# A decoder layer in float32: the normalisation factors of two layer boundaries spread by two float32r products in place of one float32 product, with the work around them in another order

## The chip, the cores and the metric

The kernel runs on one core of a Trainium2 chip. The core has a matrix engine (TensorE, "PE" in the profile; its weight loads are listed as "PEld"), three engines for elementwise work (VectorE "DVE", ScalarE "ACT", GpSimd "POOL") and DMA queues, of which SyncE ("SP") issues most. Each engine works through its own list of instructions in the order in which the program has them; between engines semaphores say when an operand is ready. The metric is the device time of one execution in microseconds (us), lower is better.

## What is computed

One layer of a decoder on 512 tokens of 1024 features, in float32: a gated feed-forward layer (FFN), a token mixer, and another FFN. Each has an RMS normalisation ahead of it and one behind it:

```python
for l in range(DEPTH):                       # DEPTH = 1
    x = x + 0.5 * rms_norm(swiglu(rms_norm(x, ffn1_pre_g[l]), ...), ffn1_post_g[l])
    y = hybrid_mixer(rms_norm(x, mix_pre_g[l]), ...)
    x = x + rms_norm(y, mix_post_g[l])
    x = x + 0.5 * rms_norm(swiglu(rms_norm(x, ffn2_pre_g[l]), ...), ffn2_post_g[l])

def rms_norm(x, g):
    return x * rsqrt(mean(x * x, axis=-1, keepdims=True) + 1e-6) * g
```

The mixer projects the 1024 features to an RG-LRU branch, its gate, and queries, keys and values, and ends in a 1024x1024 product `w_o`. What follows is about the two **boundaries**: from the output of the first FFN to the input of the mixer, and from the output of the mixer to the input of the second FFN. There a block's output `y` is normalised, added to the residual stream `xT`, and the next block's input is made from the sum.

## The kernel before

Activations lie transposed: a tile has 128 features on the partitions and the 512 tokens along the free axis, so `y`, `xT` and the next input are eight **chunks** (0 to 7) of 128 features each. The tokens come in two halves of 256 (`HALF`).

**Products.** A float32 product is made of three products in float32r, a rounded form of float32: each operand is split into a high part (rounded to float32r) and a low part (what is left), and high*high, high*low and low*high are added up in PSUM (`mm3`, lines 512 to 514). For weights ScalarE makes the high part (a CAST, line 210) and VectorE or GpSimd subtracts it for the low part (line 215). The class `Weights` holds these units in the order of their use; `W.fill(n)` has the casts and subtractions of the next n units issued at that point of the program, `W.round()` only the next cast. A unit whose low part is `shared` is cast in two halves, and VectorE and GpSimd take half of the subtraction each (line 195).

**A boundary** (`boundary`, called once per boundary; `parts` is given at the first and None at the second). The last three chunks of `y` (5, 6, 7; `late`) are computed first for token half 0 and then for token half 1, each as a product of 18 matmuls (first boundary) or 24 (second) of 256 columns. After each, VectorE copies or adds the result into `y` (`late`), ScalarE squares it (`late_square`), and VectorE adds the square to a running sum (`late_add`). When the sum of a half is complete, the class `InvRms` takes four steps:

- `stats`: TensorE sums the squares over the 128 partitions with a column of 1/1024 (`mean_d`, line 558; a float32 product, so each call runs as two instructions, four for the half);
- `invert`: ScalarE takes the square root (line 564), VectorE the reciprocal (line 566), and VectorE writes two 128x128 diagonal matrices of the factors, `dg`, beside each other (line 568);
- `spread`: TensorE multiplies a 128x128 matrix of ones by `dg` (line 572), which puts the factor of each token on every partition. This product is float32 too, and runs as two instructions of 256 columns;
- per chunk: VectorE scales `y` by gain and factor (`scale`, line 749), VectorE (even chunks) or GpSimd (odd chunks) adds it to `xT` (`add`, line 753), ScalarE makes the high part of the next input `xh` from it (`high`, line 618), and later VectorE the low part `xl` (line 621).

TensorE then starts the first four products of the next block (tiles `an` at the first boundary, `mn` at the second) with the high parts alone, chunk by chunk (`k_high`, lines 530 and 531: eight matmuls per chunk): chunks 0 to 3 of token half 0, the `stats` of half 1, chunks 4 and 5, the `spread` of half 1, chunks 6 and 7, and then all eight chunks of half 1. The low parts follow (`k_low`, line 537).

In the kernel before, `stats` of half 0 stands in the middle of the product of chunk 6, half 1, and `spread` of half 0 ahead of the product of chunk 7, half 1. Behind the spread the chunks go in pairs: two scales, the VectorE add, then the two high parts. The order of all this is the order of the Python code: nothing reorders the instructions of an engine.

## Time and profile before

| what | value |
| --- | --- |
| device time, three runs | 836.93, 837.26, 837.74 us (median 837.26) |
| device time of the profiled execution | 837.42 us |
| its span, from the first to the last instruction | 835.6 us |
| TensorE busy | 827.5 us, 99% of the span |
| VectorE, ScalarE, GpSimd busy | 732.7, 518.8, 165.9 us |
| granted TensorE clock, mean | 0.998 |
| the first boundary's late products and first next products | about 328 to 366 us of the span |
| the second boundary's | about 480 to 523 us |

A row of the timeline has the start, the duration, the engine, the line and operation, and the tiles written and read; in brackets stands the idle time ahead of it and what ended that. Rows of equal instructions that follow each other are merged (x2, x4), with the time from the first start to the last end. TensorE's matmuls overlap: a 256-column matmul is listed with 0.28 us, but one starts every 0.12 us, so what a product costs is read from the distance of starts. Line numbers in the text are those of the kernel before.

### The profile page before, as it was taken

The page shows a single profiled execution, that of the slowest core. Times are in us where ns is not written, and L with a number is a line of the kernel's source. Part 1 is how long each engine was busy: PE and PEld are TensorE (multiplying, and loading weights), DVE is VectorE, ACT ScalarE, POOL GpSimd, SP SyncE. Part 2 cuts the span into 40 slices and gives each one's busy share as a digit, 9 for nine tenths or more (in the row PEclk, how much of TensorE's full clock was granted, in tenths as well). Part 3 has the DMA queues.
Part 4 walks back from the last instruction along what each step waited for, and adds up shares of the span by engine and source line. Part 5 has one row for each costly group of instructions (what it writes and reads, how often), then busy time and mean ns, then how long its engine had stood idle before and what let it go on. Part 6 is the DMA issues. An engine that isn't in the chain of part 4 may idle for free.

```text
span 835.6 us, 11875 instructions
## 1 busy us (share of the span) xinstructions
PE 827.5 (99%) x4244; PEld 704.3 (84%) x4244; DVE 732.7 (88%) x1035; ACT 518.8 (62%) x806; POOL 165.9 (20%) x188
## 2 busy tenths in 40 slices
PE   9999999999999999999999999999999999999996
PEld 8988888888888898987788899888888888888885
DVE  4989799998989977888789689998999799898996
ACT  6656756676666654556897446545757677676562
POOL 2022000140320325414521052002005023032001
PEclk9999999999999999999999999999999999999999
DMA  7376408398595897522511140566339939769742
GB/s 253 103 272 231 151 12 308 89 266 259 128 260 179 187 282 244 170 79 93 167 42 51 51 130 23 126 176 253 118 110 243 311 91 256 234 156 259 301 141 101
DMA packets 121851, 144.22 MB, mean 173 GB/s; under 512 B 24184, under 2 KB 76736, under 8 KB 121280
## 3 DMA queue, kind: packets, MB, share of 16 engines
q1 hardware_dynamic: 107824, 112.91, 42.2%
q0 software_dynamic: 13824, 30.42, 16.6%
q8 instruction: 33, 0.54, 0.3%
q14 instruction: 26, 0.21, 0.1%
q10 hardware_dynamic: 144, 0.13, 0.0%
HBM read 100.45 MB, written 39.32 MB: 167 GB/s over the span
## 4 chain that ended last, share of the span: by engine, by line
PE 98%; DMA 1%; DVE 0%; SPq 0%; issue 0%; DVEq 0%
PE aa L999 10%; PE ab L999 10%; PE db L999 5%; PE da L999 5%; PE yaa L1390 3%; PE ba L999 3%; PE bb L999 3%; PE ya L1390 3%; PE yda L1390 2%; PE aa L929 1%; PE a_first L1260 1%; PE yab L1981 1%; PE yab L1979 1%; PE yab L1980 1%; PE wo L1905 1%; PE gt L512 1%
## 5 line engine op out<-in xcount | busy, mean ns | idle before, releaser
L1171 POOL DMA_DIRECT2D yr_a<-stage x36 | 31.6, 1020 | 176.5 <-ACT stage L1168 156.0
L1171 POOL DMA_DIRECT2D yp_b<-stage x42 | 36.5, 1065 | 146.8 <-ACT stage L1168 118.4
L1995 POOL DMA_DIRECT2D yp_b<-stage x8 | 4.3, 546 | 64.9 <-ACT stage L1994 64.4
L722 POOL TENSOR_TENSOR acca_r<-acca_r,sq_r 128x512 f32<-128x512 f32 x6 | 8.6, 1430 | 39.7 <-ACT sq_r L542 39.6
L530 PE MATMUL an<-xh_mx,whi_xl 128*128 128x256 f32 x64 | 15.9, 289 | 0.0
L531 PE MATMUL an<-xh_mx,wlo_xl 128*128 128x256 f32 x64 | 15.5, 283 | 0.0
L2098 POOL TENSOR_TENSOR last<-yp,grow 128x512 f32<-128x512 f32 x3 | 3.9, 1292 | 56.5 <-DVE yp L2088 56.5
L2095 ACT ACTIVATE ysq<-yp 128x512 f32<-128x512 f32 (+1 forms) x8 | 4.9, 607 | 15.7 <-DVE yp L2088 15.7
L512 PE MATMUL gt<-xh_mx,whi_gt 128*128 128x512 f32 x32 | 14.3, 446 | 0.0
L1427 POOL DMA_DIRECT2D yp_a<-zy x16 | 8.7, 554 | 25.0 <-DMA rows_a<-yr_a 16.7
L512 PE MATMUL pq<-xh_mx,whi_q 128*128 128x512 f32 x32 | 12.8, 401 | 0.0
L514 PE MATMUL gt<-xh_mx,wlo_gt 128*128 128x512 f32 x32 | 12.6, 394 | 0.0
L512 PE MATMUL pgb<-xh_f,whi_bg 128*128 128x512 f32 x32 | 12.6, 393 | 0.0
L513 PE MATMUL gt<-xl_mx,whi_gt 128*128 128x512 f32 x32 | 12.5, 391 | 0.0
L514 PE MATMUL pq<-xh_mx,wlo_q 128*128 128x512 f32 x32 | 12.5, 391 | 0.0
L514 PE MATMUL pgb<-xh_f,wlo_bg 128*128 128x512 f32 x32 | 12.5, 390 | 0.0
L514 PE MATMUL pub<-xh_f,wlo_bu 128*128 128x512 f32 x32 | 12.5, 390 | 0.0
L513 PE MATMUL pq<-xl_mx,whi_q 128*128 128x512 f32 x32 | 12.5, 390 | 0.0
L513 PE MATMUL pub<-xl_f,whi_bu 128*128 128x512 f32 x32 | 12.5, 390 | 0.0
L512 PE MATMUL pub<-xh_f,whi_bu 128*128 128x512 f32 x32 | 12.5, 390 | 0.0
L513 PE MATMUL pgb<-xl_f,whi_bg 128*128 128x512 f32 x32 | 12.5, 389 | 0.0
L1390 PE MATMUL ya<-whi_ad,hha 128*128 128x512 f32 x32 | 12.5, 389 | 0.0
(2038 smaller groups left out, 3414.3 us busy)
## 6 DMA issues: line engine op xcount, KB each, us to landing
yp_b<-stage POOLq DMA_DIRECT2D x50, 256.0 KB, 9.0
yr_a<-stage POOLq DMA_DIRECT2D x44, 256.0 KB, 9.6
h_a<-za SPq DMA_DIRECT2D x16, 256.0 KB
h_b<-zb SPq DMA_DIRECT2D x16, 256.0 KB
hxb<-h_b SPq DMA_DIRECT2D x16, 256.0 KB
hxa<-h_a SPq DMA_DIRECT2D x6, 512.0 KB
xn<-in_x SPq DMA_DIRECT2D x8, 256.0 KB
raw_ad<-in_ffn_w_down SPq DMA_DIRECT2D x2, 1024.0 KB
```

The lines of the kernel that those rows point to most:

```text
L512: pe.matmul(ps, hi[:, k, :], xh, start=start, stop=False)
L513: pe.matmul(ps, hi[:, k, :], xl, start=False, stop=False)
L514: pe.matmul(ps, lo[:, k, :], xh, start=False, stop=stop)
L530: pe.matmul(ps[:, sl], hi[:, k, :], xh, start=k == 0 and not goes_on, stop=False, skip_group_check=True)
L531: pe.matmul(ps[:, sl], lo[:, k, :], xh, start=False, stop=False, skip_group_check=True)
L722: eng.tensor_add(acc, acc, square(part, ALL, f"{self.name}{c}"))
L929: pe.matmul(o, w[:, k, js], x, start=first and i + j + k == 0, stop=k == 3 and i == 2, skip_group_check=True)
L999: pe.matmul(b[tb], x[:, blk], w[:, k, :], start=first and q + k + j == 0, stop=q + k == 2 and j == 2, skip_group_check=True)
L1171: pool.dma_start(o, st, accum_op=ALU.add)
L1260: pe.matmul(banks[j][:, HALF[0]], ws[j][part][:, k, :], n1.xs[k][xpart][:, HALF[0]], start=k == 0 and part == xpart, stop=stop and k == KD ...
L1390: pe.matmul(o, x[:, blk], a[:, k, :], start=start and j == 0, stop=stop and j == 2, skip_group_check=True)
L1427: (pool if q % 2 else sync).dma_start(chunks[32 * q:32 * (q + 1), :, i * P:(i + 1) * P], turned[32 * i:32 * (i + 1), :, q])
```

## The change

All of it concerns the two boundaries.

1. `invert` also rounds the factor to float32r (`rh`), subtracts (`rl`), and writes two diagonals into one tile: that of the factor (rounded on writing) and that of its rest. `spread` is two float32r products with ones, summed in PSUM.
2. At the second boundary, for half 0, the sum of squares itself is split into a high and a low part (`apart`: a ScalarE cast and a VectorE subtraction), and `stats` is four float32r products with a two-column `mean_r`.
3. The spread of half 0 moves two steps of k (six matmuls) into the product of chunk 7, half 1 (`SPREAD = 2`). Right behind it chunk 0 alone is scaled, added and rounded, then chunk 1; the result of chunk 6 is copied and squared after chunk 1's scale. Pairs are taken apart in both halves: scale, add and high part of an even chunk, then those of the odd chunk.
4. At the first boundary `W.fill(4)` moves from behind `stats` of half 0 to the start of that product. At the second `W.round` is put there, so the last unit is cast ahead of `stats`, and the fill stays behind.
5. The weights of the second FFN's first two chunks (`bg`, `bu`; four units): before, VectorE subtracts one and GpSimd three; now VectorE subtracts three and half of the fourth, GpSimd the other half.

The diff, cut to its core:

```diff
+SPREAD = 2
...
-        g, u = (add_cols(w_gu[:, :, o:o + F], f, KD, f"{name}{s}", 0, (dve, dve) if f else (dve if s == "g" else pool, pool))
-                for s, o in (("g", 0), ("u", F)))
+        lows = {"g": (dve, pool), "u": (pool, pool)} if name == "a" and not f else {"g": (dve, dve), "u": (dve, dve if f else shared)}
+        g, u = (add_cols(w_gu[:, :, o:o + F], f, KD, f"{name}{s}", 0, lows[s]) for s, o in (("g", 0), ("u", F)))
...
         def stats(self):
...
+                if self.two:
+                    for j, a in enumerate(self.two):
+                        pe.matmul(ps[:, 2 * i:2 * i + 2], a[:, i * P:(i + 1) * P], mean_r, start=j == 0, stop=j == 1)
+                    continue
...
+        def apart(self):
+            a = self.accs[0][:, HALF[self.half]]
+            t = wt(f"two_{self.name}", T, F32R)
+            self.two = hi, lo = t[:, HALF[0]], t[:, HALF[1]]
+            act.copy(hi, a)
+            dve.tensor_sub(lo, a, hi.bitcast(F32))
...
             dve.reciprocal(rs, rms)
-            self.dg = wt(f"dg_{n}", T)[:, :2 * P].rearrange("p (a b) -> p a b", a=2)
-            dve.tensor_tensor(self.dg, ident.unsqueeze(1).to_broadcast([P, 2, P]), rs.unsqueeze(2).to_broadcast([P, 2, P]), op=ALU.mult)
+            dve.tensor_copy(high, rs)
+            dve.tensor_sub(low, rs, high.bitcast(F32))
+            self.dg = wt(f"dg_{n}", T, F32R)
+            for d, r in zip(HALF, (rs, low)):
+                dve.tensor_tensor(self.dg[:, d].rearrange("p (a b) -> p a b", a=2), ident.unsqueeze(1).to_broadcast([P, 2, P]),
+                                  r.unsqueeze(2).to_broadcast([P, 2, P]), op=ALU.mult)
 
         def spread(self):
             o = self.ps[:, T // 2:]
-            pe.matmul(o, ones.bitcast(F32), self.dg.rearrange("p a b -> p (a b)"), start=True, stop=True)
+            for i, d in enumerate(HALF):
+                pe.matmul(o, ones, self.dg[:, d], start=i == 0, stop=i == 1)
...
+            if i == LATE - 1 and parts is None:
+                res.rms[0].apart()
             W.fill((2, 3, 3)[i])
...
-        def spread_a():
+        def first():
             spread(0)
-            steps((0, 1), 0, bcs[0])
-
-        n = len(xs)
-        hooks = [{}, {n // 2: res.rms[0].stats, n // 2 + 1: lambda: W.fill(4)}, {0: spread_a}]
+            step(0, 0, dve)
+            nxt.high(0, 0)
+            res.scale(1, 0, bcs[0])
+            after(1)
+            add(1, 0, pool)
+            nxt.high(1, 0)
+
+        fill = lambda: W.fill(4)
+        hooks = [{}, {1: fill, n // 2: res.rms[0].stats} if parts else {1: W.round, n // 2: res.rms[0].stats, n // 2 + 1: fill}, {SPREAD: first}]
...
         spread(1)
         for k in range(0, KD, 2):
-            steps((k, k + 1), 1, bcs[1])
+            step(k, 1, dve)
+            nxt.high(k, 1)
+            res.scale(k + 1, 1, bcs[1])
+            add(k + 1, 1, pool)
+            nxt.high(k + 1, 1)
```

Here `step(k, h, eng)` is a scale and an add, and `after(i)` the copy and the square of late chunk i.

How this moves instructions is shown at three places. First ScalarE at the first boundary, from the square of chunk 5, half 1 (`sq_r`), to the first high parts (`xh_mx`); `rms_sr` is the square root, `whi_xl` a weight's high part. Before:

```order
L542 ACTIVATE sq_r_3353<-yp_a_3131 128x256
L564 ACTIVATE rms_sr_3369<-rms_r_3366,eps 128x2
L210 CAST whi_xl_1_3378<-raw_xl__3185 128x512 x2
L542 ACTIVATE sq_r_3394<-yp_a_3131 128x256
L618 ACTIVATE xh_mx_3243<-xT_3180,cols 128x256
L618 ACTIVATE xh_mx_3245<-xT_3180,cols 128x256
```

And now, on the same engine at the same place:

```order
L545 ACTIVATE sq_r_3355<-yp_a_3133 128x256
L211 CAST whi_xl_1_3362<-raw_xl__3187 128x512 x2
L580 ACTIVATE rms_sr_3380<-rms_r_3377,eps 128x2
L638 ACTIVATE xh_mx_3245<-xT_3182,cols 128x256
L545 ACTIVATE sq_r_3414<-yp_a_3133 128x256
L638 ACTIVATE xh_mx_3247<-xT_3182,cols 128x256
L638 ACTIVATE xh_mx_3249<-xT_3182,cols 128x256
```

The two casts now stand ahead of the square root, and the first high part ahead of the square of chunk 6. Second, VectorE at the same place, from the running sum (`accb_r`) to the first add into `xT`; `rs_r` is the reciprocal, `wlo_xl` the VectorE half of a weight's low part. Before:

```order
L741 TENSOR_TENSOR accb_r_3066<-acca_r_3065,sq_r_3353 128x256
L566 RECIPROCAL rs_r_3371<-rms_sr_3369 128x2
L568 TENSOR_TENSOR dg_r_3373<-ident,rs_r_3371 128x256
L195 TENSOR_TENSOR wlo_xl_1_3379<-raw_xl__3185,whi_xl_1_3378 128x512
L728 TENSOR_TENSOR yp_a_3131<-ay_3356,yp_a_3131 128x256
L749 SCALAR_TENSOR_TENSOR yp_a_2971<-yp_a_2971,half_g,rms_r_3366 128x256 x2
L753 TENSOR_TENSOR xT_3180<-yp_a_2971,xT_3180 128x256
```

And now, with the rounded factor `rh_r`, its rest `rl_sr` and the second diagonal:

```order
L761 TENSOR_TENSOR accb_r_3068<-acca_r_3067,sq_r_3355 128x256
L196 TENSOR_TENSOR wlo_xl_1_3363<-raw_xl__3187,whi_xl_1_3362 128x512
L581 RECIPROCAL rs_sr_3381<-rms_sr_3380 128x2
L582 CAST rh_r_3383<-rs_sr_3381 128x2
L583 TENSOR_TENSOR rl_sr_3382<-rs_sr_3381,rh_r_3383 128x2
L586 TENSOR_TENSOR dg_r_3388<-ident,rs_sr_3381 128x256
L586 TENSOR_TENSOR dg_r_3388<-ident,rl_sr_3382 128x256
L769 SCALAR_TENSOR_TENSOR yp_a_2973<-yp_a_2973,half_g,rms_r_3377 128x256
L788 TENSOR_TENSOR xT_3182<-yp_a_2973,xT_3182 128x256
L769 SCALAR_TENSOR_TENSOR yp_a_2973<-yp_a_2973,half_g,rms_r_3377 128x256
L748 TENSOR_TENSOR yp_a_3133<-ay_3358,yp_a_3133 128x256
```

The weight's half now stands ahead of the reciprocal, three instructions are new, and chunk 0's add follows its own scale. Third, VectorE at the second boundary, between the first low part (`wlo_bg_0`) and the copies of the late chunks (`y_r`). Before:

```order
L215 TENSOR_TENSOR wlo_bg_0_4930<-raw_bg__4788,whi_bg_0_4929 128x1024
L732 COPY y_r_4962<-my_4937 128x256
L745 TENSOR_TENSOR accb_r_4678<-accb_r_4678,sq_r_4964 128x256
L732 COPY y_r_4998<-my_4973 128x256
L745 TENSOR_TENSOR accb_r_4678<-accb_r_4678,sq_r_5000 128x256
L732 COPY y_r_4923<-my_5003 128x256
```

And now, where `two_r` is the low part of the sum of squares that `stats` reads:

```order
L216 TENSOR_TENSOR wlo_bg_0_4944<-raw_bg__4802,whi_bg_0_4943 128x1024
L216 TENSOR_TENSOR wlo_bu_0_4948<-raw_bu__4862,whi_bu_0_4947 128x1024
L752 COPY y_r_4976<-my_4951 128x256
L765 TENSOR_TENSOR accb_r_4692<-accb_r_4692,sq_r_4978 128x256
L216 TENSOR_TENSOR wlo_bg_1_4982<-raw_bg__4802,whi_bg_1_4981 128x1024
L752 COPY y_r_5012<-my_4987 128x256
L765 TENSOR_TENSOR accb_r_4692<-accb_r_4692,sq_r_5014 128x256
L574 TENSOR_TENSOR two_r_5017<-accb_r_4692,two_r_5017 128x256
L752 COPY y_r_4937<-my_5020 128x256
```

Two low parts that GpSimd had stand between the copies now, and a subtraction follows the last sum.

More of the change, by code (lines that the diff above doesn't have):

```diff
@@ L482, in tile_layer @@
     mean_c = filled("mean_c", 1, 1.0 / C)
+    mean_r = const.tile([P, 2], F32R, name="mean_r")
+    dve.memset(mean_r.bitcast(F32), 1.0 / D)
     eps = filled("eps", 1, EPS)
@@ L550, in __init__ @@
         def __init__(self, accs, mean, half, name, eps=eps):
-            self.accs, self.mean, self.half, self.name, self.eps = accs, mean, half, name, eps
+            self.accs, self.mean, self.half, self.name, self.eps, self.two = accs, mean, half, name, eps, None
         def stats(self):
@@ L761, in boundary, with add, step @@
             res.late_add(0, i == 0)
+            if i == LATE - 1 and parts is None:
+                res.rms[0].apart()
             W.fill((2, 3, 3)[i])
-        def steps(ks, h, bc):
-            for k in ks:
-                res.scale(k, h, bc)
-            for k in ks:
-                res.add(k, h)
-            for k in ks:
-                nxt.high(k, h)
+        def add(k, h, eng):
+            sl = HALF[h]
+            eng.tensor_add(xT[k][:, sl], res.ys[k][:, sl], xT[k][:, sl])
+        def step(k, h, eng):
+            res.scale(k, h, bcs[h])
+            add(k, h, eng)
         bcs = [None, None]
```

39 lines of the change are left out of this document (20 added, 19 removed).

## The prediction

> **What bounds the kernel now.** I read the page's engine shares first, then the list of TensorE's waits, then the timelines of the four engines at the two boundaries.
>
> ```profile
> PE 827.5 (99%) x4244; PEld 704.3 (84%) x4244; DVE 732.7 (88%) x1035; ACT 518.8 (62%) x806; POOL 165.9 (20%) x188
> PE warm L1247 <- POOL ident masks.py:199: 1.4, 1, 1.4
> PE xtp L1195 <- DMA xn<-in_x: 0.4, 1, 0.4
> ```
>
> TensorE is the bound: it is busy for 99% of the span, and its only listed waits (total, times, longest) are 1.4 and 0.4 us, both at the start. So a change can win only what TensorE itself spends on the pieces that are changed, plus waits too short to be listed, which show as a wider distance between two matmul starts. And each wait that the change puts in front of TensorE is paid in full.
>
> What TensorE spends on a spread, and on its small waits:
>
> ```profile
> 505.27 0.28 PE L531 MATMUL mn<-xh_f,wlo_bu 128*128 128x256 f32 x1
> 505.39 0.59 PE L572 MATMUL rms_r<-dg_r,ones 128*128 128x256 f32 x2
> 505.94 0.28 PE L531 MATMUL mn<-xh_f,wlo_bg 128*128 128x256 f32 x1
> 507.61 0.28 PE L531 MATMUL mn<-xh_f,wlo_bu 128*128 128x256 f32 x1
> 507.83 0.39 PE L530 MATMUL mn<-xh_f,whi_bg 128*128 128x256 f32 x1
> 508.05 0.28 PE L531 MATMUL mn<-xh_f,wlo_bg 128*128 128x256 f32 x1
> 494.00 0.50 PE L558 MATMUL rms_r<-mean_d,accb_r 128*128 128x1 f32 x4
> 494.57 0.28 PE L513 MATMUL my<-attn,whi_wo 128*128 128x256 f32 x1
> 339.25 0.28 PE L514 MATMUL ay<-hha,wlo_ad 128*128 128x256 f32 x1
> 339.46 0.67 PE L572 MATMUL rms_r<-dg_r,ones 128*128 128x256 f32 x2
> ```
>
> A float32r matmul of 256 columns takes one slot of 0.12 us (505.27 to 505.39). From the spread's start to the second matmul behind it are 0.55 us, of which one slot is an ordinary matmul's: the float32 spread costs 0.43. The statistics cost 0.57 - 0.12 = 0.45 in the same way. Where half 1's first high part is late (507.83) the two distances are 0.22 instead of 0.12: a wait of 0.10 and another 0.10 until the pipeline is full again, 0.20 in all. At 339.46 the spread comes 0.09 after its slot.
>
> **The savings.** Two float32r matmuls are 0.24, so each of the four spreads saves 0.19, together 0.76. No row has a float32r matmul of two columns; four of them lie between nothing and four slots (0.48, no gain). I take 0.30, nearer the four float32 instructions (0.45) because the count is the same: 0.15 saved, once. If every small wait went too (0.10 to 0.16 at the first spread, 0.20 twice, 0.03 elsewhere), 1.5 us would be won: that is the ceiling, 0.18% of the time. All else is what the chain from statistics to high parts does. It must be followed four times. These rows carry its durations:
>
> ```profile
> 526.88 0.18 DVE L593 RECIPROCAL rs_nf<-rms_nf 128x4 f32<-128x4 f32 x1 [1.03 <-ACT rms_nf L592]
> 527.38 0.69 DVE L598 TENSOR_TENSOR dh_nf<-ident,rs_nf 128x512 fp32r<-128x512 f32 x1
> 337.49 0.42 ACT L542 ACTIVATE sq_r<-yp_a 128x256 f32<-128x256 f32 x1 [0.92 <-DVE yp_a L728]
> 338.39 0.26 ACT L564 ACTIVATE rms_sr<-rms_r,eps 128x2 f32<-128x2 f32 x1 [0.48 <-PE rms_r L558]
> 338.55 1.13 ACT L210 CAST whi_xl<-raw_xl__3185 128x512 fp32r<-128x512 f32 x2
> 338.89 0.43 DVE L568 TENSOR_TENSOR dg_r<-ident,rs_r 128x256 f32<-128x256 f32 x1
> 339.23 0.69 DVE L195 TENSOR_TENSOR wlo_xl<-raw_xl__3185,whi_xl 128x512 fp32r<-128x512 f32 x1
> 339.76 1.31 POOL L195 TENSOR_TENSOR wlo_xl<-raw_xl__3185,whi_xl 128x512 fp32r<-128x512 f32 x1 [8.44 <-ACT whi_xl L210]
> 340.17 0.88 DVE L749 SCALAR_TENSOR_TENSOR yp_a<-yp_a,half_g,rms_r 128x256 f32<-128x256 f32 x2
> 340.95 0.42 DVE L753 TENSOR_TENSOR xT<-yp_a,xT 128x256 f32<-128x256 f32 x1
> 341.12 0.86 POOL L753 TENSOR_TENSOR xT<-yp_a,xT 128x256 f32<-128x256 f32 x1
> 341.41 0.51 ACT L618 ACTIVATE xh_mx<-xT,cols 128x256 fp32r<-128x256 f32 x1 [0.65 <-DVE xT L753]
> 342.11 0.28 PE L530 MATMUL an<-xh_mx,whi_xl 128*128 128x256 f32 x1
> ```
>
> The normalisation of a whole block (first two rows) already does what the change does: from reciprocal to first diagonal 0.50. The next VectorE instruction starts 0.34 after a 256-column diagonal (338.89 to 339.23), so the second diagonal ends 0.50 + 0.34 + 0.43 = 1.27 after the reciprocal's start, against 0.63 now. From a diagonal's end (339.32) to TensorE's start on it are 0.14, from a high part (0.49) to TensorE 0.07 (350.19 and 350.75, below), between VectorE and ScalarE 0.04, to GpSimd 0.08, and an instruction that needs the one ahead of it on VectorE starts 0.03 after its end.
>
> **First boundary, half 0.** The casts now stand ahead of the square root: 337.49 + 0.32 = 337.81, casts until 338.94, square root until 339.16 instead of 338.65. VectorE's half of the weight (from 338.45) fits ahead of the reciprocal at 339.20. Without further waits the second diagonal ends at 340.47 and TensorE has it at 340.61. TensorE's slot for it: the third product starts at 339.37, six matmuls on is 340.09, the second spread matmul 340.21. So TensorE waits 0.40 where it waited 0.09.
>
> But GpSimd's half of the weight now starts with the second cast, 339.00, and runs to 340.31, beside the subtraction and the diagonals. What that does to VectorE, rows of the second boundary show:
>
> ```profile
> 487.32 1.23 DVE L215 TENSOR_TENSOR wlo_bg<-raw_bg__4788,whi_bg 128x1024 fp32r<-128x1024 f32 x1 [0.52 <-ACT whi_bg L210]
> 488.31 2.50 POOL L215 TENSOR_TENSOR wlo_bu<-raw_bu__4848,whi_bu 128x1024 fp32r<-128x1024 f32 x1 [3.36 <-ACT whi_bu L210]
> 488.46 0.42 DVE L732 COPY y_r<-my 128x256 f32<-128x256 f32 x1
> 489.43 1.67 DVE L745 TENSOR_TENSOR accb_r<-accb_r,sq_r 128x256 f32<-128x256 f32 x1 [0.54 <-ACT sq_r L542]
> 491.92 1.73 DVE L745 TENSOR_TENSOR accb_r<-accb_r,sq_r 128x256 f32<-128x256 f32 x1 [0.48 <-ACT sq_r L542]
> 488.97 0.42 ACT L542 ACTIVATE sq_r<-y_r 128x256 f32<-128x256 f32 x1 [0.74 <-DVE y_r L732]
> 489.30 1.04 ACT L210 CAST whi_bg<-raw_bg__4788 128x1024 fp32r<-128x1024 f32 x1
> ```
>
> An add of two SBUF tiles, 0.42 by itself, takes 1.67 and 1.73 beside a GpSimd subtraction, and ends 0.29 after GpSimd's end (491.10, 490.81). The copy from PSUM beside it is not held. The new subtraction of two columns and the two diagonals also read two SBUF tiles; nothing in the trace shows such small ones beside GpSimd. Bounds: not held (second diagonal ends 340.47), or held like the adds: subtraction ends 340.60, diagonals 340.52 to 341.30. I take held, since the instruction is the same kind.
>
> [...]
>
> Held, then: TensorE's second spread matmul at 341.44, spread done 341.72, scale 341.76, add 342.27, high part 342.73 to 343.22, chunk 0 on TensorE at 343.29 instead of 342.11. Chunk 1: its scale stands behind chunk 0's add (+0.34) at 342.61, GpSimd 343.17 to 344.03, high part until 344.56, TensorE 344.63; it would want chunk 1 at 343.29 + 0.10 + 8 slots = 344.35. With the refill chunk 1 flows at 344.73, against 342.11 + 0.96 = 343.07: **+1.66**. Not held, all of this is 0.83 less: **+0.83**. Later chunks come ahead of their slots. Moving `first` past the sum's adds delays nobody: half 1's sum is due only at its statistics, after four chunks of 0.96 us.
>
> **Half 1, either boundary**, counted from its statistics:
>
> ```profile
> 345.95 0.51 PE L558 MATMUL rms_r<-mean_d,accb_r 128*128 128x1 f32 x4
> 346.79 0.17 DVE L566 RECIPROCAL rs_r<-rms_sr 128x2 f32<-128x2 f32 x1 [0.81 <-ACT rms_sr L564]
> 347.34 1.27 DVE L621 SCALAR_TENSOR_TENSOR xl_mx<-xT,cols,xh_mx 128x256 fp32r<-128x256 f32 x3
> 348.94 0.87 DVE L749 SCALAR_TENSOR_TENSOR yp_a<-yp_a,half_g,rms_r 128x256 f32<-128x256 f32 x2 [0.34 <-PE rms_r L572]
> 350.19 4.47 ACT L618 ACTIVATE xh_mx<-xT,cols 128x256 fp32r<-128x256 f32 x8 [2.63 <-DVE xT L753]
> 350.75 0.39 PE L530 MATMUL an<-xh_mx,whi_xl 128*128 128x256 f32 x1
> ```
>
> Reciprocal +0.84, second diagonal +1.68 to +2.11: the spread's slot at +2.36 is met. But three low parts (0.40 each) now end so that the first scale starts at +3.23, not +2.99. Add +3.74, high part +4.20 to +4.69, TensorE +4.76, where it is now +4.80: chunk 0's earlier add just makes up for it, and the 0.19 saved at the spread becomes a wait here. Chunk 1: scale +4.08, GpSimd +4.64 to +5.50, high part until +6.03, TensorE +6.10; wanted at 4.76 + 0.10 + 0.96 = +5.82. Now the pair's two scales come first, GpSimd starts 0.95 after the first scale instead of 1.41, and chunk 1 is in time. It flows at +6.20 instead of 4.90 + 0.96 = +5.86: **+0.34** per boundary, 0.68.
>
> **Second boundary, half 0.** VectorE: low part 487.32, the second one 488.46, copy 489.60, square 490.06 to 490.48, add 490.52. ScalarE casts 0.33 after the square, 490.39 to 491.43, so the third low part is 491.47, the copy of chunk 7 492.61, square until 493.49, last add until 493.96: only 0.31 later than now, as the two adds lose their 1.3 us each. But cast and subtraction of the sum follow (0.42 + 0.43 and two hand-overs): 494.89, on TensorE 495.03 instead of 494.00. **A wait of 1.03.** Behind it copy (494.80) and square of chunk 5 (495.26), two casts (495.58 to 496.71), then the square root, reciprocal 496.96, second diagonal 498.23, TensorE 498.37; held by GpSimd's half (496.77 to 498.08) 499.06, TensorE 499.20. TensorE's own slot: 495.03 + 0.30 + 0.10 + 18 x 0.12 + 0.12 = 497.71. So it waits 1.49 (0.66). 18 matmuls, 0.12 and a refill later the next products begin: 501.58 (500.75). Before:
>
> ```profile
> 499.17 0.31 PE L530 MATMUL mn<-xh_f,whi_bg 128*128 128x256 f32 x1
> ```
>
> **+2.41** (not held **+1.58**). Chunks 0 and 1 are ready at 501.1 and 502.45, ahead of their slots. The memset of `mean_r` lies in VectorE's idle start and costs nothing; no DMA changes its place in a queue.
>
> **Sum.** 1.66 + 0.68 + 2.41 = 4.75, or 0.83 + 0.68 + 1.58 = 3.09. The savings are in these, since slots were counted with 0.12. The profiled execution took 837.42, 0.16 above the median of 837.26: 837.42 + 4.75 = 842.2, against the median 842.0.
>
> **Rivals.** (a) The small VectorE instructions are not held by GpSimd: 837.3 + 3.1 = 840.4. For it speaks that no row shows a 0.16 us subtraction held; against it the two adds. (b) No slower: TensorE finds each diagonal ready and takes the savings, at best 837.3 - 1.5 = 835.8. That needs the second diagonal by 340.07 at the first boundary (I have 340.47 at the earliest), the split sum by 493.86 (494.89) and the diagonal by 496.4 at the second. For it: VectorE is relieved of 2.6 us of held adds there, and if the low parts came behind the copies the sum would be ready at 493. Against it: the order puts 2.3 us of low parts between them. It decides once those waits shrink by about 1 us each. (c) More than the sum: GpSimd's adds of the odd chunks hold VectorE's adds of the even ones so long that chunks 2, 4 and 6 come late too, another 0.3 in each of the four halves, 843.2. For it: they now overlap; against it: by my times these chunks are about 0.5 to 1 us ahead of their slots.
>
> **Chances.** The forecast, held, 0.5; (a) 0.27; (b), wholly or most of the way, 0.17; (c) 0.06. Predicted: 842.0. The range goes from between (a) and (b), 838.9, to (c), 843.2. A difference under 0.2% (1.7 us) is about what a measurement of this kernel cannot tell from none; (b) lies inside that even at its best, so faster by more has 0.03, no change 0.15, and slower, (a), (c) and the forecast, 0.82.
>
> **What would show it.** In the profile after: the first boundary's spread starting near 341 instead of 339.46, with the two-column subtraction stretched to about 1 us (right) or at 0.16 (rival a); the second's statistics near 495.0 and spread near 499; distances of 0.3 to 0.4 ahead of chunk 1 of half 1; two spread matmuls 0.12 apart. Wrong if ScalarE's casts or VectorE's low parts start earlier than I place them, because an engine's list is not the limit that I take it for.

## The result, and the profile after

| | before | after |
| --- | --- | --- |
| device time, median | 837.47 us | 847.5 us |
| runs | 836.93, 837.26, 837.68, 837.74 | 846.72, 847.38, 847.61, 848.5 |
| ratio, 95% interval | | 1.012 (1.0107 to 1.0133) |
| profiled execution, span | 837.42, 835.6 | 846.72, 844.7 |

It became slower by 10.0 us where 4.75 were forecast; the range given ended at 843.2. The page's shares of the engines and the head of its chain of work, after:

```profile
PE 830.7 (98%) x4244; PEld 703.7 (83%) x4244; DVE 736.9 (87%) x1052; ACT 512.9 (61%) x808; POOL 159.6 (19%) x186
...
PE 86%; DVE 7%; DMA 3%; ACT 2%; issue 1%; SPq 0%; POOL 0%; DVEq 0%; ACTq 0%
```

TensorE does about the same work (busy for 830.7 us, 827.5 before) in a span 9.1 us longer, so it waits. For what, the list of its waits after says (us in total, times, longest):

```profile
PE rms_r L592 <- DVE dg_r L586: 1.8, 2, 1.1
PE warm L1281 <- POOL ident masks.py:199: 1.4, 1, 1.4
PE ydb L2015 <- DVE hla L916: 1.0, 1, 1.0
PE ya L515 <- ACT hha L970: 0.8, 1, 0.8
PE yaa L1424 <- ACT stage L1202: 0.6, 1, 0.6
PE an L533 <- ACT xh_mx L638: 0.3, 2, 0.2
PE rms_r L562 <- ACT two_r L573: 0.3, 1, 0.3
PE xtp L1229 <- DMA xn<-in_x: 0.3, 1, 0.3
PE aa L1033 <- ACT ba L1038: 0.3, 1, 0.3
PE rms_r L562 <- DVE two_r L574: 0.2, 1, 0.2
```

The waits on `dg_r`, `two_r` and `xh_mx` are the boundaries', as forecast. Those on `ydb`, `ya`, `yaa` and `aa` are not: they lie in the two FFNs, where the change alters no instruction. (Lines after stand 1 to 34 higher than before; `ya` at L515 is L512 before.)

To see where time is lost, the start of TensorE's n-th matmul after is compared with that before, both from the span's start. The growth of this lag, in us, by stage (the halves are those of the tokens; the last columns are all that lies outside the boundaries; the other kernels are explained below):

```
              first boundary    second boundary   in the      up to first  between  behind
              half 0  half 1    half 0  half 1    boundaries  boundary     them     second
forecast       1.66    0.34      2.41    0.34       4.75
after          1.44    0.29      2.17    0.26       4.16        3.06       -0.41     2.00
a0             1.43    0.30      2.17    0.25       4.15       -0.49        0.05    -0.02
p32           -0.01    0.01     -0.02    0.01      -0.01        2.09       -0.43     0.77
p64            0.00    0.00     -0.01    0.00      -0.01        0.89        0.00     1.98
order          1.21   -0.03      1.03   -0.03       2.18        0.18       -0.40     0.00
pair           1.65    0.18      0.12    0.21       2.16        0.02        0.08     0.00
f32stat        1.43    0.31      1.29    0.27       3.30       -0.14        0.05     0.00
rec2           1.23    0.17      1.96    0.12       3.48        0.22        0.06    -0.02
late_fill      1.31    0.28      1.44    0.39       3.42        0.94        0.02    -0.03
best           1.31    0.29      0.55    0.45       2.60        0.78        0.05     0.00
pool3          1.43    0.31      2.83    0.23       4.80        0.24        0.07    -0.03
```

Up to about 1 us outside the boundaries means nothing here: `f32stat` and `late_fill`, with medians of 841.12 and 841.25 us, have -0.14 and 0.94 ahead of the first boundary, `order` and `pair`, with 839.80 and 839.81, have -0.40 and 0.08 between the two. Inside the boundaries the forecast of 4.75 stands against 4.16. The other half of the loss, 3.06 and 2.00, is in the FFNs. A row shows one execution, the profiled one: that of `p32` took 839.97 us, the least of its six (median 842.11), so its row holds about half of what `p32` loses.

The first boundary, half 0, in the timelines of TensorE, VectorE and GpSimd after:

```profile
340.91 0.50 PE L565 MATMUL rms_r<-mean_d,accb_r 128*128 128x1 f32 x4
342.08 1.29 POOL L196 TENSOR_TENSOR wlo_xl<-raw_xl__3187,whi_xl 128x512 fp32r<-128x512 f32 x1 [7.16 <-ACT whi_xl L211]
342.19 0.17 DVE L581 RECIPROCAL rs_sr<-rms_sr 128x2 f32<-128x2 f32 x1
342.39 1.00 DVE L582 CAST rh_r<-rs_sr 128x2 fp32r<-128x2 f32 x1
343.42 0.16 DVE L583 TENSOR_TENSOR rl_sr<-rs_sr,rh_r 128x2 f32<-128x2 f32 x1
344.07 0.63 PE L592 MATMUL rms_r<-dg_r,ones 128*128 128x256 f32 x2 [0.76 <-DVE dg_r L586]
346.27 0.39 PE L533 MATMUL an<-xh_mx,whi_xl 128*128 128x256 f32 x1 [0.15 <-ACT xh_mx L638]
```

From statistics to chunk 0 it takes 5.36 us instead of 4.26. It is the cast of two columns that is held, until GpSimd is done (343.39 and 343.37), not the subtraction behind it. The second boundary's statistics, spread and first product after:

```profile
498.84 0.27 PE L562 MATMUL rms_r<-mean_r,two_r 128*128 128x2 f32 x1 [0.30 <-ACT two_r L573]
499.31 0.49 PE L562 MATMUL rms_r<-mean_r,two_r 128*128 128x2 f32 x3 [0.19 <-DVE two_r L574]
503.13 0.63 PE L592 MATMUL rms_r<-dg_r,ones 128*128 128x256 f32 x2 [1.08 <-DVE dg_r L586]
505.75 0.28 PE L533 MATMUL mn<-xh_f,whi_bg 128*128 128x256 f32 x1
```

Then the FFN. What TensorE waits for there goes back to a transfer that lands late. VectorE's addition of a weight's parts, first before and then after:

```profile
174.23 1.23 DVE L296 TENSOR_TENSOR raw_ax__1490<-raw_ay__1673,raw_ax__1490 128x1024 f32<-128x1024 f32 x1
```

```profile
180.38 1.23 DVE L297 TENSOR_TENSOR raw_ax__1492<-raw_ay__1675,raw_ax__1492 128x1024 f32<-128x1024 f32 x1 [5.20 <-DMA raw_ay__1675<-in_ffn_w_gu]
```

VectorE stands still for 5.2 us there and runs late after it, as it does again 58 us later, with the next weight (4.5 us). ScalarE's copies of TensorE's results (`stage`) stand behind casts that wait for VectorE. After, at the wait on `yaa`, the cast, then the copies, then TensorE:

```profile
284.80 1.05 ACT L251 CAST whi_aq__2696<-raw_ax__2472 128x1024 fp32r<-128x1024 f32 x1 [1.52 <-DVE raw_ax__2472 L260]
...
285.75 1.07 ACT L1202 COPY stage<-yaa 128x512 f32<-128x512 f32 x2
...
286.38 0.50 PE L1424 MATMUL yaa<-whi_adv__2643,hhs 128*128 128x512 f32 x1 [0.64 <-ACT stage L1202]
```

Ahead of the late weight in SyncE's queue is `h_a<-za`, made of 512-byte packets. SyncE's issues of it (duration in ns: shortest, median, longest), before and then after:

```profile
L1013 SPq DMA_DIRECT2D h_a<-za x16: 327/558/1245, 123.4 to 276.1; - x16
```

```profile
L1047 SPq DMA_DIRECT2D h_a<-za x16: 327/758/1452, 123.5 to 279.3; - x16
```

The same issues of the same transfers take a median of 758 ns instead of 558. What has changed for them is their place: the new constant `mean_r`, 8 bytes of each partition, is given a slot of 32 ahead of all pools but its own, and the activations (pool `big`), the weights (`wpool`) and the work tiles (`tmp`) all lie 32 bytes further on: at byte 18464 instead of 18432 (72 x 256), 114720 instead of 114688, 204832 instead of 204800.

### The profile page after: what moved, and what is told of

It is laid out like the page before. It is cut to its first block, busy times and chain, and to the rows that moved or that the text cites. A ratio compares the mean times of both kernels' runs of the same rounds, so it can differ in the third digit from the quotient of the medians.

```text
span 844.7 us, 11893 instructions
## 1 busy us (share of the span) xinstructions
PE 830.7 (98%) x4244; PEld 703.7 (83%) x4244; DVE 736.9 (87%) x1052; ACT 512.9 (61%) x808; POOL 159.6 (19%) x186
## 4 chain that ended last, share of the span: by engine, by line
PE 86%; DVE 7%; DMA 3%; ACT 2%; issue 1%; SPq 0%; POOL 0%; DVEq 0%; ACTq 0%
PE aa L1033 10%; PE ab L1033 10%; PE da L1033 5%; PE db L1033 5%; PE yaa L1424 3%; PE bb L1033 3%; PE ba L1033 3%; PE ya L1424 3%; PE yda L1424 2%; PE a_first L1294 1%; DMA rows_a<-yr_a 1%; PE wo L1939 1%; PE yab L2013 1%; PE yab L2015 1%; PE yab L2014 1%
## 5 line engine op out<-in xcount | busy, mean ns | idle before, releaser
L1205 POOL DMA_DIRECT2D yr_a<-stage x36 | 31.7, 1015 | 178.3 <-ACT stage L1202 155.2
L515 PE MATMUL gt<-xh_mx,whi_gt 128*128 128x512 f32 x32 | 14.3, 446 | 0.0
L638 ACT ACTIVATE xh_f<-xT,cols 128x256 fp32r<-128x256 f32 x16 | 7.6, 505 | 9.8 <-DVE xT L788 6.1
L638 ACT ACTIVATE xh_mx<-xT,cols 128x256 fp32r<-128x256 f32 x16 | 7.6, 504 | 9.7 <-DVE xT L788 6.1
L533 PEld LDWEIGHTS an<-xh_mx,whi_xl 128*128 128x128 f32 x64 | 12.2, 191 | 1.1 <-ACT xh_mx L638 1.1
L515 PE MATMUL pq<-xh_mx,whi_q 128*128 128x512 f32 x32 | 12.8, 400 | 0.0
L515 PE MATMUL ya<-hha,whi_ad 128*128 128x512 f32 x30 | 11.8, 394 | 0.8 <-ACT hha L970 0.8
L515 PE MATMUL pgb<-xh_f,whi_bg 128*128 128x512 f32 x32 | 12.6, 393 | 0.0
L515 PE MATMUL pub<-xh_f,whi_bu 128*128 128x512 f32 x32 | 12.5, 389 | 0.0
```

What stands on the lines that cost most here:

```text
L515: pe.matmul(ps, hi[:, k, :], xh, start=start, stop=False)
L533: pe.matmul(ps[:, sl], hi[:, k, :], xh, start=k == 0 and not goes_on, stop=False, skip_group_check=True)
L638: act.activation(x[0][:, sl], src, AF.Copy, scale=gain)
L1205: pool.dma_start(o, st, accum_op=ALU.add)
```

## Experiments

Two theories. **Place**: half of the loss comes from these 32 bytes, the other half from the boundaries' waits. **Order**: all of it comes from the changed instructions, the waits in the FFNs too.

### The place of the tiles

`p32`, `p64` and `p256` are the kernel before with a constant that nothing reads (2, 16 or 64 columns); `a0` is the kernel after with `mean_d` read from `mean_r`, which moves the tiles back:

```diff
 p32, on the kernel before
     mean_c = filled("mean_c", 1, 1.0 / C)
+    filled("unused", 2, 1.0 / D)
 a0, on the kernel after
-    mean_d = filled("mean_d", 1, 1.0 / D)
+    mean_r = const.tile([P, 2], F32R, name="mean_r")
+    dve.memset(mean_r.bitcast(F32), 1.0 / D)
+    mean_d = mean_r.bitcast(F32)[:, 0:1]
```

> The kernel before with one more constant of two columns that nothing reads (a memset in VectorE's idle start). It takes 32 bytes of each partition, so every tile behind the constants lies 32 bytes further on, as in the kernel after. Theory place: about 4.9 us of the 10 us come from that alone, through longer DMA packets: 842 to 843 us, the 512-byte packets of h_a<-za at about 35 instead of 32 ns, VectorE's add on raw_ay__1675's counterpart near 180 instead of 174 us, and TensorE waits on ydb, ya and yaa of 0.6 to 1.0 us. Rival order: the loss outside the boundaries comes from the change's own instructions: no change, 837.4 us.

> The same with a constant of 64 bytes. If the grain of the effect is 64 bytes, as before: 837.4 us, packets of 32 ns. If what counts is that a tile starts on a multiple of 256 bytes (before it does), 842 to 843 us as with 32 bytes. Rival order: 837.4.

> The same with a constant of 256 bytes, which keeps every tile's start on a multiple of 256 bytes. Theory place: 837.4 us, packets of 32 ns. If any move of the tiles costs, whatever its size (another pattern of buffers), slower as with 32 bytes. Rival order: 837.4.

> The kernel after, with the one-column constant mean_d read from the new two-column one, so that no tile is moved; every instruction stays but one memset. Theory place: only the boundaries' own waits are left, by the lags of the two traces 1.9 at the first and 2.2 at the second: 837.4 + 4.1 = 841.5 us, and no wait on yaa, ya or ydb. Rival order: 847.5 us as the kernel after.

| kernel | median us | ratio to before, interval |
| --- | --- | --- |
| p32 | 842.11 (839.97 to 845.49) | 1.0071 (1.0057 to 1.0086) |
| p64 | 840.26 | 1.0039 (1.0027 to 1.0051) |
| p256 | 837.08 | 1.0001 (0.9993 to 1.0010) |
| a0 | 841.51 | 1.0057 (1.0045 to 1.0069) |

Place holds: an unread constant costs 5.1 us (before had 837.04 in these runs; by the interval 4.8 to 7.2), one of 256 bytes nothing, and the change without its 32 bytes costs 4.5. Together 9.5, of the 10.0 measured. `p64` lies between its two numbers, 3.2 us over before. So in these kernels a move by 256 bytes is free and one by 32 or 64 is not; 128 was not run. TensorE's waits in `p32`, whose boundaries are those of before:

```profile
PE warm L1248 <- POOL ident masks.py:199: 1.4, 1, 1.4
PE ya L513 <- ACT hha L937: 1.1, 1, 1.1
PE ya L514 <- DVE hla L869: 0.6, 1, 0.6
PE ydb L1982 <- DVE hla L883: 0.3, 1, 0.3
```

And in `a0`, where none of those is left:

```profile
PE rms_r L592 <- DVE dg_r L586: 1.8, 2, 1.1
PE warm L1281 <- POOL ident masks.py:199: 1.4, 1, 1.4
PE rms_r L562 <- ACT two_r L573: 0.3, 1, 0.3
PE an L533 <- ACT xh_mx L638: 0.2, 1, 0.2
PE rms_r L562 <- DVE two_r L574: 0.2, 1, 0.2
```

The issues of `h_a<-za` in `p32`, then in `p256`:

```profile
L1014 SPq DMA_DIRECT2D h_a<-za x16: 327/760/1453, 122.9 to 276.2; - x16
```

```profile
L1014 SPq DMA_DIRECT2D h_a<-za x16: 327/560/1245, 123.0 to 275.7; - x16
```

The packets' own records say the same: between 160 and 180 us the 2048 packets of 512 bytes took 31.7 ns in the mean before, 36.1 in `p32`, 36.0 in `p64`, 36.1 after, 31.8 in `p256`, 31.7 in `a0`. That is 14% longer where the tiles are moved by 32 or 64 bytes, and no longer where they are moved by 256. Why, no trace shows.

The longer packets alone are not 5 us: 2048 packets of 4.4 ns more, spread over the 16 DMA engines of the page, are an estimated 0.56 us, and SyncE's four issues of `h_a<-za` ahead of the late weight do take 3.43 us instead of 2.83, in `p32` and after alike. How 0.6 us there becomes 3.5 to 5.2 us of VectorE's waiting for the weight is not shown; GpSimd's stores `yr_a<-stage`, issued from 165.24 after and 164.25 before, come while SyncE issues that weight (164.88 to 167.72 and 163.31 to 165.50), and take a median of 11.1 us from issue to landing after (the four issued from 162 to 168 us) and 8.8 before (the three from 161 to 166.5).

### Which tiles?

The gap between two pools moves the activations alone (`big32`, `big64`) or all but the activations (`rest32`, `rest64`; `rest256` as a control):

```diff
 rest32, on the kernel before (rest64: 16 columns, rest256: 64)
     big = ctx.enter_context(tc.tile_pool(name="big", bufs=1))
+    gap = ctx.enter_context(tc.tile_pool(name="gap", bufs=1))
...
+    dve.memset(gap.tile([P, 8], F32, name="gap"), 0.0)
 big32: gap of 56 columns, and the unread constant of p32 (big64: 48 and 16 columns)
```

> The kernel before; only the pool of activations (the tiles of h_a<-za, hxa<-h_a, the input and the first weights, where the 512-byte packets are) lies 32 bytes further on, the weights and the work tiles lie 256 further on. Theory place, by the packets: the 512-byte ones are the ones that grew most, so most of p32's 5 us: 840 to 842. If the stores of stage or the weights' loads matter most: 837.5 to 838.

> The kernel before with the weights, the work tiles and all behind them 32 bytes further on, and the activations where they were. Theory place, by the packets: packets of 2048 bytes grew little, so little of the 5 us: 837.3 to 838.5. If the weights' loads or the stores matter most: 840 to 842.

> As rest32, with 64 bytes instead of 32 between the activations and the weights. Theory: what made every 512-column matmul of big32 and rest32 start 0.233 instead of 0.227 us after the one ahead is that weights and activations lie apart by an odd multiple of 32 bytes more than before; by 64 the distance is 0.227 again, and the time is near before: 837 to 839 us. Rival: any gap between the two pools does it (or the pool itself): 854 us.

> As rest32 with 256 bytes. Theory: neither packets nor matmuls change, 837.4 us. Rival, the additional pool itself: 854 us.

> Activations 64 bytes further on, weights and work tiles 256 further on: they lie apart by 192 bytes more than before. Theory: matmuls at 0.227 us, and the 512-byte packets at 35 ns as in p64 and big32; since p64 had 3.2 us by moving everything, this one should have most of it: 839.5 to 841 us, with the wait on ydb, while rest64 has little. Rival for the gap: 854 us; rival for the packets (the stores and weight loads carry p64's loss): 837.5 and rest64 840.

| kernel | activations moved by | weights and work tiles by | median us | ratio, interval |
| --- | --- | --- | --- | --- |
| big32 | 32 | 256 | 853.97 | 1.0196 (1.0182 to 1.0210) |
| rest32 | 0 | 32 | 854.29 | 1.0201 (1.0187 to 1.0215) |
| big64 | 64 | 256 | 851.03 | 1.0171 (1.0157 to 1.0185) |
| rest64 | 0 | 64 | 850.36 | 1.0156 (1.0139 to 1.0174) |
| rest256 | 0 | 256 | 837.49 | 1.0002 (0.9993 to 1.0011) |

No expectation of mine foresaw the first two, and the theory formed from them (odd multiples of 32 bytes) fell with the next two, which came near their rivals' 854; `rest256` shows that it is not the additional pool itself. In all four slow kernels TensorE's only listed waits are at the start of the program, but each 512-column matmul starts 0.2333 us after the one ahead, instead of 0.2267 (mean distance of TensorE's starts between 140 and 160 us). Rows of windows of before and then of `rest32` (busy time with the number of matmuls in 20 us, granted clock, DMA share, GB/s):

```profile
140.00:160.00 20.00, 20.00 (x90) 1.00 0.40 142
200.00:220.00 20.00, 20.00 (x89) 1.00 0.31 109
```

```profile
140.00:160.00 20.00, 20.00 (x87) 1.00 0.55 201
200.00:220.00 20.00, 20.00 (x87) 1.00 0.42 148
```

So 87 matmuls fit where 90 did, at the same clock. `p32` and `p64`, which move all pools together, keep 0.2267, and so does `rest256`. What the slow ones share is the distance between the activations and what lies behind them (weights and work tiles, which moved together here), changed by 32, 64, 192 or 224 bytes. Why, is open; it is not that every matmul takes longer, since those of 256 columns (tile `aa`) start every 0.114 to 0.118 us in the four, and every 0.120 before.

These kernels therefore say nothing on the device time that either pool's transfers cost, as TensorE's slowness hides it. The packets do speak: with the activations moved the 512-byte packets take 36.0 and 36.5 ns (`big32`, `big64`), with the rest moved 31.7. The issues of `h_a<-za` in `big32`, then `rest32`:

```profile
L1016 SPq DMA_DIRECT2D h_a<-za x16: 327/758/1452, 125.0 to 282.3; - x16
```

```profile
L1015 SPq DMA_DIRECT2D h_a<-za x16: 327/557/1252, 125.6 to 282.5; - x16
```

VectorE's waits for the late weights say the same. These are its five waits for a weight's part (`raw_ay`, `raw_by`) in the two FFNs, in order of time, in us; a dash is a wait that is not listed:

```
before, p256      -    -    -    -    -
rest256           -   0.6   -    -    -
a0               0.7  1.0   -    -    -
rest32           0.8  1.2  0.3  0.3   -
rest64           0.9  1.0   -   0.3   -
big32            3.7  4.0  3.9  4.0  3.6
big64            2.3  4.3  2.3  4.2  4.0
p32              3.5  3.7  3.9  3.8  3.7
p64              2.6  3.9  2.0  3.9  4.8
after            5.2  4.5  3.7  3.9  5.1
```

`big32` and `rest32` have the same slow TensorE and nearly the same time, and only the first has the long waits. So the weights come late when the activations are moved off their place, whether the weights themselves lie on a multiple of 256 bytes (`big32`, `big64`) or not (`p32`, `p64`): 2.0 to 4.8 us each. Moving the weights alone does not do it: at most 1.2 (`rest32`, `rest64`), where `a0` has up to 1.0.

### Inside the boundaries

All but `pair` are built on `a0`, so their time is read against its 4.5 us.

```diff
 order: old invert, spread and stats (one diagonal, float32); order and low parts of the change
 pair, on the kernel before: only the new invert and spread
 f32stat
-            if i == LATE - 1 and parts is None:
-                res.rms[0].apart()
 rec2
-            dve.tensor_copy(high, rs)
+            with nc.allow_low_precision(reason="high part"):
+                dve.reciprocal(high, rms)
 late_fill (best: late_fill and f32stat together)
-        hooks = [{}, {1: fill, n // 2: res.rms[0].stats} if parts else {1: W.round, n // 2: res.rms[0].stats, n // 2 + 1: fill}, {SPREAD: first}]
+        hooks = [{}, {n // 2: res.rms[0].stats, n // 2 + 1: fill}, {SPREAD: first}]
 pool3: low parts dealt as before
+        lows = {"g": (dve, dve if f else pool), "u": (dve, dve) if f else (pool, pool)}
```

> As a0 with the spread and the statistics in float32 as before (one diagonal, no rounded factor, no split): what is left is the order (chunk 0 first, spread two k-steps later, fill ahead of the statistics) and the low parts moved to VectorE. Theory: the order costs 0.5 us at the first boundary, since the spread stands 0.72 us later and chunk 0's chain is only some 0.4 us shorter, and 0 to 0.5 at the second: 837.5 to 838 us, so that some 3.5 of a0's 4.5 us belong to the float32r pair and the split. Rival: the order and the low parts cost most of it: above 840 us.

> The kernel before with the float32r pair alone: rounded factor, its rest, two diagonals, two spread matmuls; order, low parts and statistics as before, no tile of a transfer moved. Theory: the later diagonals push VectorE's half of the weight beside GpSimd's at the first boundary, and chunk 0 comes 1.5 us later there; half 1 costs 0.5 at either boundary, less 0.2 saved at the second's half 0: 837.4 + 2.3 = 839.7 us. With order's 2.3 that makes about a0's 4.5. Rival: the pair's costs were only a matter of the change's order, and by itself it wins its four times 0.19: 836.6 us.

> As a0 without the split of the sum of squares at the second boundary: no cast two_r, no subtraction, and the statistics of half 0 as a float32 product. Theory: the split is what makes the statistics late, by its cast 0.40, subtraction 0.43 and hand-overs; without it they start 0.1 us after their slot, and all behind them is 0.6 to 0.7 us sooner: 840.8 us. Rival: the low parts that VectorE has taken over make the sum late anyway: 841.5 us less nothing, the wait then named for the last add.

> As a0 (the change without its 32-byte move), but the rounded factor rh is written by a second reciprocal instead of by the cast of two columns. In a0 that cast takes 1.00 us at half 0 of both boundaries and ends with GpSimd's half of the weight, while the reciprocal ahead of it and the subtraction behind it take 0.17 and 0.16. Theory: it is the cast that GpSimd holds, and a reciprocal is not held: both spreads come 0.8 us sooner, TensorE's waits of 0.76 and 1.08 shrink to about 0 and 0.3, and the time falls from 841.5 by 1.5 to 840.0 us. Rival: whatever small instruction comes next is held until GpSimd is done (the subtraction takes the 1 us then): 841.5 us.

> As a0 with the fills behind the statistics at both boundaries, as in the kernel before (part 4 of the change undone). GpSimd's half of the weight then starts after the diagonals are written. Theory: what makes the spreads late is that half beside the inversion; without it the cast takes 0.17, the second diagonal is ready 0.8 us sooner at the first boundary and 1.2 at the second (the square root no longer stands behind the casts either), both spreads find their slots, and 1.9 us of a0's 4.5 go: about 839.5 us. Rival: VectorE's half of the weight then stands between the diagonals and chunk 0's scale and costs as much: 841 us or more.

> As late_fill, also without the split of the sum of squares. Theory: another 0.7 us less, 838.5 to 839 us, with no wait of TensorE on a diagonal or on the statistics over 0.2 us; what is left over the 837.2 of before is the later place of the first boundary's spread and the two halves 1 of 0.3 each. Rival: with all waits gone the four float32r spreads win: below 837 us.

> As a0 with the low parts of bg and bu dealt as before: VectorE one, GpSimd three. Theory: GpSimd's subtractions of 2.5 us hold VectorE's adds at the second boundary again, and the last of them holds the cast of the factor for some 2 us instead of 1: the spread there waits 1 to 2 us longer than in a0, 842.5 to 843.5 us. Rival: the low parts on VectorE are what makes the second boundary late, and without them it gains: below 841 us.

| kernel | median us | before in these runs | ratio, interval |
| --- | --- | --- | --- |
| order | 839.80 | 837.52 | 1.0028 (1.0017 to 1.0038) |
| pair | 839.81 | 837.23 | 1.0033 (1.0020 to 1.0046) |
| f32stat | 841.12 | 837.52 | 1.0046 (1.0033 to 1.0060) |
| rec2 | 841.45 | 837.52 | 1.0049 (1.0036 to 1.0061) |
| late_fill | 841.25 | 837.43 | 1.0045 (1.0031 to 1.0058) |
| best | 840.45 | 837.43 | 1.0037 (1.0025 to 1.0050) |
| pool3 | 842.87 | 837.52 | 1.0068 (1.0056 to 1.0081) |

**order** lies between its two expectations (2.3 us over before): the order costs more than twice the 0.5 to 1.0 that I gave it. The single diagonal is held as well, and TensorE waits 1.2 us in all for the two of half 0; the rest of the 2.2 by the lags is not explained. The first boundary's row, with GpSimd's half beside it, takes 1.26 us, where before it took 0.43:

```profile
339.51 1.26 DVE L582 TENSOR_TENSOR dg_r<-ident,rs_sr 128x256 f32<-128x256 f32 x1
```

**pair** came out as expected in sum, 2.6 us over before, and at the first boundary's half 0 (1.65); the halves 1 cost 0.18 and 0.21, not 0.5. So neither order nor pair wins anything alone. Their losses do not simply add up: both together, without the split of the sum, are `f32stat`, 3.6 us over before, less than 2.3 + 2.6. In `pair` GpSimd's half starts at 339.77, near the end of the last diagonal (339.94), and it is VectorE's half, beside it, that is held (1.78 us, 0.69 before) and then keeps the scale waiting:

```profile
339.86 1.78 DVE L195 TENSOR_TENSOR wlo_xl<-raw_xl__3185,whi_xl 128x512 fp32r<-128x512 f32 x1
```

**late_fill** missed for that reason, and its rival held at the first boundary (1.31 by the lags, 1.43 in `a0`); at the second 0.73 is gained (1.44 instead of 2.17). Its spreads do find their slots, but VectorE's half now takes 1.79 us between the diagonals and chunk 0's scale, and TensorE waits for chunk 0 instead:

```profile
PE an L533 <- ACT xh_mx L638: 1.4, 2, 1.2
...
PE mn L533 <- ACT xh_f L638: 0.5, 2, 0.3
```

**rec2** fell for the rival: the second reciprocal is not held, and the subtraction behind it is. The first boundary in it:

```profile
339.43 0.14 DVE L583 RECIPROCAL rh_r<-rms_sr 128x2 fp32r<-128x2 f32 x1
339.61 0.93 DVE L584 TENSOR_TENSOR rl_sr<-rs_sr,rh_r 128x2 f32<-128x2 f32 x1
```

What is gained is 0.2 us at each half 0 and 0.13 at each half 1 by the table of lags, which the medians cannot resolve. Beside a GpSimd subtraction, then, the cast is held (1.00 in `a0`) and so is the subtraction (0.93), and the reciprocal is not: at the second boundary of `rec2` GpSimd's half runs from 498.44 to 499.72, and the second reciprocal starts at 498.63 and takes 0.14. What sets the reciprocal apart from the cast, which has one input too, no run here shows.

**f32stat** gains 0.88 at the second boundary's half 0 by the lags (2.17 to 1.29), a little more than expected: the split of the sum costs more than it saves. **pool3** is as expected: with a whole low part on GpSimd the cast waits for all of it, 2.08 us:

```profile
498.70 2.08 DVE L582 CAST rh_r<-rs_sr 128x2 fp32r<-128x2 f32 x1
```

**best** met neither number. No wait for a diagonal or for the statistics is left, as expected, but those for chunk 0 are as in `late_fill` (1.4 us at the first boundary), which neither number had counted. It has the least loss of the variants that keep both the pair and chunk 0's order, and is still 3 us over before. No version beat the kernel before.

## Why the prediction was wrong

**The step that failed** is the one at the end of the second boundary's part: "The memset of `mean_r` lies in VectorE's idle start and costs nothing; no DMA changes its place in a queue." The memset does cost nothing (with one more, `p256` has 837.08 us against 837.04 before), but the constant moved every tile behind it by 32 bytes. `p32`, which has nothing else of the change, costs 5.1 us, with the 512-byte packets at 36.1 instead of 31.7 ns and VectorE waiting 3.5 to 3.9 us for each of five weights. No instruction of the boundaries has a part in it. The way from the packets to the 5.1 us is argued, not shown in full. All terms, rivals and both ends of the range lay inside the two boundaries; no case had a loss elsewhere, so the upper end of 843.2 could not hold it.

**Inside the boundaries** the forecast was of the right kind and 0.3 to 0.6 us too large: 4.75 against 4.5 by `a0`'s median and 4.15 by the lags.

- First boundary, half 0: +1.66 forecast, +1.44. That a small instruction is held was right, which one was wrong: the cast, which I had not counted among those held because it has one input. It ends 0.02 after GpSimd, not 0.29 after; counted from the statistics, the spread came about 0.3 sooner than forecast and chunk 1 about 0.2, which is the difference.
- Halves 1: +0.34 each, measured +0.29 and +0.26; chunk 0's earlier add and chunk 1's small wait are as described.
- Second boundary, half 0: +2.41 forecast, +2.17. The waits are where they were put: on the split sum (0.30 on the high and 0.19 on the low part by the list, where one wait of 1.03 was forecast), then on the diagonal (1.08 by the list, 1.49 forecast). The float32r statistics save nothing: the last three of the four start at 499.31 and the next product 0.35 later (0.36 in `a0`), so each takes a slot of 0.12, 0.48 in all against 0.45. I had taken 0.30.
- A pair of spread matmuls takes two slots, as forecast: in half 1 after, where nothing waits for the diagonal, the next product starts 0.24 (352.81) and 0.23 us (511.95) after the pair.

**The rivals.** (a), nothing held, falls with the cast's 1.00 us and, for the subtraction, with the 0.93 in `rec2`. (b), no waits, falls with the waits on `dg_r`. (c) happens and is harmless: VectorE's adds beside GpSimd's take 0.67 instead of 0.42 in half 1 of `a0`, but later chunks do not come late.

**Still open**: how longer packets of the activations make the weights late by several us, how much of the 5 us each pool's transfers carry, why the distance of the pools slows TensorE's 512-column matmuls, and why `p64`, with packets as long as in `p32`, loses less (3.2) and mostly behind the second boundary.

## What to carry to other kernels

Before a change is priced, compare the addresses of all tiles, not the instructions alone: a constant of 8 bytes, placed ahead of the large pools, cost as much here (5.1 us in `p32`) as all the rest of the change together (4.5 in `a0`). In these kernels only moves by 256 bytes were free (`p256` 837.08 us against 837.04 before, `rest256` 837.49 against 837.23), so keep the pools that transfers touch at such a place and distance, or let one constant serve for two, as `a0` does. Where VectorE and GpSimd share a weight's low part near a chain of tiny instructions, look at which link of the chain runs beside GpSimd's half: moving that part earlier or later only changed here which one was held, the cast in `a0` (1.00 us), VectorE's half in `late_fill` (1.79).

## What the runs showed that I had not expected

- 512-byte packets of `h_a<-za` take 36 instead of 31.7 ns when the activations lie 32 or 64 bytes further on than before (31.8 at 256), and VectorE waits 2.0 to 4.8 us for each of five weights in `p32` and `p64`; moving all pools costs 5.1 us (32 bytes) and 3.2 us (64) of device time, in a kernel whose TensorE is busy for 99%.
- TensorE's 512-column float32r matmuls start every 0.2333 instead of 0.2267 us, at the same granted clock, when activations and what lies behind them are 32, 64, 192 or 224 bytes further apart than before; at 256 more they do not (`rest256`, 0.2267). That is 1.6 to 2.0% of the whole time.
- A float32r matmul of two columns takes the same slot of 0.12 us as one of 256 columns: from the start of three of them to the next product are 0.35 us after and 0.36 in `a0`.
- A cast of 128x2 on VectorE takes 0.99 to 2.08 us beside a subtraction on GpSimd (`a0`, `pool3`), and 0.17 without it (`late_fill`); a reciprocal of the same size takes 0.14 beside it (`rec2`).
